# Dilated attention of one mixer: both heads of a unit in turn, scaling on ScalarE, values and the first pair's keys and queries ahead of the mixing

## The chip, the cores and the metric

One Trainium2 chip; the kernel runs on one of its cores. The metric is device time in microseconds, median of several executions. The engines are named as the profile names them: PE (TensorE, matmuls), DVE (VectorE), ACT (ScalarE), POOL (GpSimd), SP (the queue that issues DMAs). Each engine works through its own instructions in order; between engines they wait on semaphores.

## The reference, cut to what matters

Eight layers' halves run one after the other on a (512 tokens, 1024 features) activation. The change lies in one of them, the "even" mixer:

```python
def even_mixer(h, w_in, a_ln_g, a_ln_b, a_ws, a_bs, q_g, k_g, w_out):
    u, v, q, k, vb = split(h @ w_in, [512, 1024, 1536, 2048])
    a_out = chunked_gmlp(gelu(u), gelu(v), a_ln_g, a_ln_b, a_ws, a_bs)   # layer norm of v, causal mixing by a_ws
    qh = rms_norm(heads(q), q_g); kh = rms_norm(heads(k), k_g); vh = heads(vb)   # 8 heads of 64
    for window, dilation in ((128, 1), (512, 4), (2048, 16)):
        o_r, l_r = dilated_branch(qh, kh, vh, window, dilation)   # softmax in the branch's keys
    o = sum over branches of softmax(l_r) * o_r
    return concatenate([a_out, o], -1) @ w_out
```

The kernel computes the three branches at once: a key that lies in n branches counts n times, so that one softmax over all causal keys, with the weight `cnt` (0 to 3) multiplied onto each exponential, gives the same result.

## The kernel before, in words

Activations lie feature by token: 8 tiles of 128x512. Every matrix product is done in three passes (high part times high part, high times low, low times high), so a 128-column block of a projection is 24 matmuls of 512 columns (`mm3`, lines 239 to 241). A weight block is loaded by SP into one of two raw buffers, ACT writes its high part (L213) and DVE the low part (L214). All instructions are written down in a program order, and then a list scheduler puts each engine's instructions into an order of its own from its estimate of the times; what an engine does in which order is therefore not the order of the code.

The even mixer (`even`, L1389) has three parts. `gmlp` projects v by tokens (`token_proj`: 4 weight loads, 96 matmuls, into 4 PSUM banks), projects u in 4 blocks, normalises v and mixes (8 groups of three 256-column matmuls, L1257 to L1259, evicted by ACT, L1260, then 4 transposes, L1264). `dilated` treats 8 heads in 4 pairs. For each pair and each of k, q and v there is a projection of 24 matmuls (`project`, steps P0, P1, P2). For k and q the squares (ACT L1323) are summed per head by small "moments" matmuls (L1326), an inverse root is worked out on DVE in 13 dependent instructions on 128x8 values (L1345 to L1348), for k it is transposed (L1355), copied (L1357), spread over the features by a matmul with `hrow` (L1359) and multiplied in (DVE L1360). For v the projection is scaled by DVE (L1028) and transposed (L1031).

The causal scores of one pair fall into three units, `EVEN_UNITS`: unit 0 is query block 3 (512 keys), unit 1 blocks 0 and 2 (128 and 384 keys), unit 2 block 1 (256 keys). Steps: S makes both heads' scores of a unit in two PSUM banks (L1096, with the mask added by L1094), W makes the weights of one head (`weigh`: DVE maximum L1370, DVE negative scaled maximum L1372, ACT exponential L1373, DVE product with `cnt` and sum L1374, DVE reciprocal L1375, DVE scaling L1376), T transposes weights (PE L1054, ACT L1059, DVE L1060), V multiplies with the values (L1070 to L1075, ACT copy L1077, DVE add L1078). `attention` (L1099) runs the steps of the string `EVEN_STEPS` in each round; the number behind the colon says how many pairs ahead or behind the round's own pair a step works. Transposes and values of a pair stand up to two rounds behind its scores there. A pool of four PSUM banks (`aux`) serves scores, moments and transposes in turn, two banks (`mm`) the projections. Behind the last pair comes the output projection with `ev_wo` (192 matmuls), parts of which the scheduler moves forward.

Of the kernel before, what the change touches and what calls it, by code (L numbers as in the profile page):

```python
# [31 lines left out]
          + [("ba", 4), ("hg", 2)])  # L32
# [25 lines left out]
    "W01:0 S1:0 W00:0 W10:0 T01:-1 T00:0 T21:-1 V0:-2 P0:1 W11:0 S2:0 P2:0 V1:-1 W20:0 T11:0 T20:0 "  # L58
    "W21:0 T10:0 P1:1 S0:1"
# [46 lines left out]
class Kern:  # L106
# [914 lines left out]
    def values(self, ps, vz, scale=None):  # L1021

        nc = self.nc
        vt = self.scr()
        if scale is None:
            nc.scalar.activation(vt, ps, AF.Copy)
        else:
            nc.vector.tensor_mul(vt, ps, scale)  # L1028
# [3 lines left out]
        src = tr.rearrange("p (b d) -> p b d", d=64)  # L1032
        nc.scalar.activation(vz[:, :, 64:128], src, AF.Copy)
        nc.vector.tensor_sub(vz[:, :, 128:192], src, vz[:, :, 64:128])

    def value_tiles(self, n=2):
        res = []
        for k in range(n):
            t = self.pt(f"vz{k}", [P, 8, 192], F32R)
            self.nc.gpsimd.memset(t.bitcast(F32)[:, :, 0:64], 0.0)  # L1040
            res.append(t)
        return res
# [19 lines left out]
    def av(self, s, vz, wts, e):  # L1062
# [4 lines left out]
        for j in range(4):  # L1067
            h, l = (t[:, 4 * j:3 * j + 4].rearrange("p q c -> p (q c)") for t in wts)
            v = vz[:, 2 * j + e]
# [29 lines left out]
    def attention(self, pairs, first, project, weigh, done, mask, order, units):  # L1099
# [5 lines left out]
        for i in range(-2, pairs + 3):  # L1105
            for name, d in steps:
# [5 lines left out]
                if kind == "S":  # L1112
                    s["z", n] = self.scores(s["q"], s["k"], units[n], mask)
                elif kind == "W":
# [15 lines left out]
    def stick(self):  # L1130
        nc = self.nc
        with self.phase("stick") as self.ph:
# [5 lines left out]
            vzs = self.value_tiles()  # L1138
# [57 lines left out]
    def gmlp(self, oh, ol):  # L1196
# [15 lines left out]
        pv = self.token_proj([("ev_v", u) for u in range(4)], self.xh, self.xl)  # L1212
        with self.phase("big") as self.big:
            self.rms_scales()
            early(2)
            self.rms_rows(range(4))
        wr = self.load("wsr", [P, 1024], i["ev_ws"], eng=nc.sync, pool=self.ph)
# [15 lines left out]
        r = self.rstd(var, 4)  # L1233
        for n, v in enumerate(vg):
            V.tensor_scalar(v, v, ag[:, 2 * n:2 * n + 1], r[:, n:n + 1], op0=ALU.subtract, op1=ALU.mult)
# [12 lines left out]
        self.linear(bu[len(pu):], self.xh, self.xl, lambda a, pss: evict(a + len(pu), pss))  # L1248

# [24 lines left out]
    def dilated_masks(self):  # L1274

        nc = self.nc
        ps = self.aux()
        for k, n in enumerate((4, 16)):
            a = self.scr()[0:n, :P]
            nc.gpsimd.memset(a, 0.0)  # L1280
            nc.gpsimd.affine_select(a, a, pattern=[[0, P // n], [-1, n]], compare_op=ALU.not_equal, fill=1.0,
                                    base=0, channel_multiplier=1)
            nc.tensor.matmul(ps[:, :P], a, a, start=k == 0, stop=k == 1)
        cnt = self.pt("cnt")
        for j in range(4):
            nc.scalar.activation(cnt[:, j * P:(j + 1) * P], ps[:, :P], AF.Copy, bias=1.0 if j == 3 else 0.0)
        own = cnt[:, 3 * P:]
        nc.gpsimd.affine_select(own, own, pattern=[[-1, P]], compare_op=ALU.is_ge, fill=0.0, base=0,
                                channel_multiplier=1)
        near = self.scr()[:, :P]  # L1290
        nc.gpsimd.memset(near, 1.0)
        nc.gpsimd.affine_select(near, near, pattern=[[1, P]], compare_op=ALU.is_ge, fill=0.0, base=0,
                                channel_multiplier=-1)
        nc.vector.tensor_add(cnt[:, 2 * P:3 * P], cnt[:, 2 * P:3 * P], near)
        mask = self.pt("dmask", [P, T], BF16)
# [3 lines left out]
    def dilated(self, oh, ol):
        nc, i = self.nc, self.i  # L1300
        V = nc.vector
        cnt, mask = self.dilated_masks()
        gq = self.load("gq", [P, 2], i["ev_qkg"], eng=nc.sync, pool=self.ph)
        gqk = self.pt("gqk", [P, 1])
        V.tensor_mul(gqk, gq[:, 0:1], gq[:, 1:2])
        hsel = self.pt("hsel", [P, 2])
# [3 lines left out]
        hrow = self.pt("hrow", [2, P])  # L1310
        rsq = self.pt("rsq", [P, 104])[:, :4]
# [3 lines left out]
        vzs = self.value_tiles()  # L1315
        bk, bq, bv = (self.simple_blocks(n, 4) for n in ("ev_k", "ev_q", "ev_vb"))

        V.tensor_mul(rsq, self.rcol, self.rcol)

        def moments(ps, st, c0):  # L1320

            sq = self.scr()
            nc.scalar.activation(sq, ps, AF.Square)  # L1323
            for tb in range(4):
                c = c0 + 2 * tb
                nc.tensor.matmul(st[:, c:c + 2], sq[:, tb * P:(tb + 1) * P], hsel, start=True, stop=True)  # L1326

        def project(hp, s, n):

            ps, = self.group([(bk, bq, bv)[n][hp]], self.xh, self.xl)  # L1330
            if n == 2:
                s["v"] = vzs[hp % 2]
                self.values(ps, s["v"], self.rrow)
                return
            st = self.aux()
            moments(ps, st, 0)
            if n == 0:
                kr = self.scr()
                nc.scalar.activation(kr, ps, AF.Copy, scale=gqk)  # L1339
            else:  # L1340
                s["q"] = self.split_psum(ps, "q", 2)
            var = self.small(8)
            per_head = lambda t: t[:, :, None].to_broadcast([P, 4, 2])
            two = lambda t: t.rearrange("p (t e) -> p t e", e=2)
            V.tensor_tensor(two(var), two(st[:, :8]), per_head(rsq), op=ALU.mult)  # L1345
            V.tensor_scalar(var, var, 1e-6, None, op0=ALU.add)
            r = self.rstd(var, 8)
            V.tensor_tensor(two(r), two(r), per_head(self.rcol), op=ALU.mult)  # L1348
            if n == 1:
                s["rq"] = self.small(8)  # L1350
                V.tensor_scalar(s["rq"], r, 0.125, None, op0=ALU.mult)
                return
            tr = self.aux()
            for tb in range(4):
                nc.tensor.transpose(tr[0:2, tb * P:(tb + 1) * P], r[:, 2 * tb:2 * tb + 2], self.ident)  # L1355
            rt = self.pt("rt", [2, T])
            nc.scalar.activation(rt, tr[0:2], AF.Copy)  # L1357
            bc = self.aux()
            nc.tensor.matmul(bc, hrow, rt, start=True, stop=True)  # L1359
            V.tensor_mul(kr, kr, bc)  # L1360
            s["k"] = (self.pt("kh", dt=F32R, bufs=2), self.pt("kl", dt=F32R, bufs=2))
            self.split(kr, *s["k"])

        def weigh(hp, st, z, segs, e):
            p = self.scr()
            for qb, c0 in segs:
                kv = (qb + 1) * P
                zq, pq = z[:, c0:c0 + kv], p[:, c0:c0 + kv]
                mx, nb, den = self.small(1), self.small(1), self.small(1)
                V.reduce_max(mx, zq, axis=AX.X)  # L1370
                sc = st["rq"][:, 2 * qb + e:2 * qb + e + 1]
# [5 lines left out]
            return p  # L1377
# [4 lines left out]
        def first(st):  # L1382
            self.ready = [(0, 0), (0, 1), (0, 2)]
            for hp, n in self.ready:
                project(hp, st[hp], n)

        self.attention(4, first, project, weigh, done, mask, EVEN_STEPS, EVEN_UNITS)

    def even(self):  # L1389
        with self.phase("evout") as self.op:  # L1390
            oh, ol = [None] * NM, [None] * NM
            with self.phase("gmlp") as self.ph:
# [285 lines left out]
    def load_params(self):  # L1678
# [10 lines left out]
        self.ba, self.hg = col["ba"], col["hg"]  # L1689
# [56 lines left out]
def layout(inp):  # L1746
# [10 lines left out]
    par = {"ba": i["od_b_a_2"][0], "hg": i["od_head_g_2"][0]}  # L1757
    for j in (0, 1):
# [22 lines left out]
    d["ev_u"], d["ev_q"], d["ev_k"], d["ev_vb"] = (tiles(w[:, a:a + T]) for a in (0, 1024, 1536, 2048))  # L1781
# [31 lines left out]
```

## Time and profile before

| | us |
|---|---|
| median of 3 runs | 2461.49 (2459.39 to 2463.71) |
| profiled execution | 2465.87 |
| its span, first to last instruction | 2464.1 |
| PE busy in the span | 2392.6 (97%) |
| DVE, ACT busy | 1416.0 (57%), 1003.4 (41%) |

PE is busy nearly everywhere, in the sense that some matmul is under way; matmuls are pipelined and their ends are modelled, so this share hides short stalls. More is seen in the stretches of the even mixer: its first matmul starts at 1255.86 us and that of the next stage at 1502.57 us, and the granted clock of PE is below 1.00 in four of the stretches shown below.

### The profile page before, as it was taken

How to read it: one execution, taken by the hardware profiler on the slowest of the kernel's cores; microseconds unless marked ns; L12 is line 12 of the kernel's file. 1: busy time of each engine (PE TensorE's matmuls, PEld its weight loads, DVE VectorE, ACT ScalarE, POOL GpSimd, SP SyncE). 2: the span in 40 equal slices, each digit the busy share in tenths (PEclk: the TensorE clock that was granted, in tenths of full speed). 3: DMA queues.
4: the chain of work that ended last, by engine and by line, in shares of the span. 5: the costliest groups of instructions: out<-in, count | busy, mean ns of one | idle time of the engine just before them, and what ended most of it. 6: DMA issues, size and time to landing. Idle time of an engine off the chain costs nothing. (4 is left out here: it accounts for less than half of the span.)

```text
span 2464.1 us, 30835 instructions
## 1 busy us (share of the span) xinstructions
PE 2392.6 (97%) x12136; PEld 1987.2 (81%) x12140; DVE 1416.0 (57%) x2560; ACT 1003.4 (41%) x1542; POOL 19.6 (1%) x123
## 2 busy tenths in 40 slices
PE   5899999999999999999999999999999999999999
PEld 4788888888878788888877678888888887888888
DVE  9945633343787863334376886656435677655621
ACT  5843522322665643222254454333225454333311
POOL 0000000000000000000000000000000000000000
PEclk9999999999999999999999999999999999999999
DMA  3532223233221113233322112332332122223231
GB/s 90 110 102 87 86 95 102 92 94 96 78 69 61 52 61 120 94 96 93 99 92 67 44 46 86 112 100 93 94 96 86 52 87 76 94 95 102 90 113 63
DMA packets 99377, 213.49 MB, mean 87 GB/s; under 512 B 44529, under 2 KB 45169, under 8 KB 99233
## 3 DMA queue, kind: packets, MB, share of 16 engines
q1 hardware_dynamic: 99232, 211.53, 27.5%
q8 instruction: 95, 1.56, 0.3%
q14 instruction: 50, 0.40, 0.1%
HBM read 207.04 MB, written 2.10 MB: 85 GB/s over the span
## 5 line engine op out<-in xcount | busy, mean ns | idle before, releaser
L213 ACT ACTIVATE wh<-wr 128x1024 fp32r<-128x1024 f32 (+1 forms) x385 | 400.4, 1041 | 1016.4 <-PE mm L240 401.2
L214 DVE TENSOR_TENSOR wl<-wr,wh 128x1024 fp32r<-128x1024 f32 (+1 forms) x385 | 461.6, 1199 | 440.6 <-ACT wh L213 436.4
L239 PE MATMUL mm<-xh,wh 128*128 128x512 f32 x1016 | 400.5, 394 | 3.5 <-ACT scr L1339 3.1
L240 PE MATMUL mm<-xl,wh 128*128 128x512 f32 x1016 | 400.1, 394 | 0.0
L241 PE MATMUL mm<-xh,wl 128*128 128x512 f32 x1016 | 399.8, 393 | 0.0
L239 PE MATMUL acc<-xh,wh 128*128 128x512 f32 x760 | 296.4, 390 | 0.0
L240 PE MATMUL acc<-xl,wh 128*128 128x512 f32 x760 | 295.9, 389 | 0.0
L241 PE MATMUL acc<-xh,wl 128*128 128x512 f32 x760 | 295.7, 389 | 0.0
L239 PEld LDWEIGHTS mm<-xh,wh 128*128 128x128 f32 x1016 | 192.2, 189 | 45.8 <-ACT scr L1339 3.5
L240 PEld LDWEIGHTS mm<-xl,wh 128*128 128x128 f32 x1016 | 192.2, 189 | 39.6 <-issue 0.2
L241 PEld LDWEIGHTS mm<-xh,wl 128*128 128x128 f32 x1016 | 192.2, 189 | 39.2 <-issue 0.6
L239 PEld LDWEIGHTS acc<-xh,wh 128*128 128x128 f32 x760 | 142.8, 188 | 29.6
L240 PEld LDWEIGHTS acc<-xl,wh 128*128 128x128 f32 x760 | 142.8, 188 | 29.5 <-issue 0.2
L241 PEld LDWEIGHTS acc<-xh,wl 128*128 128x128 f32 x760 | 142.8, 188 | 29.3
L239 PE MATMUL mm<-hh,wh 128*128 128x512 f32 (+1 forms) x396 | 145.0, 366 | 1.0 <-DVE v L353 1.0
L239 PE MATMUL acc<-hh,wh 128*128 128x512 f32 (+1 forms) x396 | 145.1, 366 | 0.5 <-DVE v L353 0.5
L240 PE MATMUL acc<-hl,wh 128*128 128x512 f32 (+1 forms) x396 | 145.1, 366 | 0.0
L240 PE MATMUL mm<-hl,wh 128*128 128x512 f32 (+1 forms) x396 | 145.0, 366 | 0.0
L241 PE MATMUL mm<-hh,wl 128*128 128x512 f32 (+1 forms) x396 | 144.7, 365 | 0.0
L241 PE MATMUL acc<-hh,wl 128*128 128x512 f32 (+1 forms) x396 | 144.7, 365 | 0.0
L239 PEld LDWEIGHTS mm<-hh,wh 128*128 128x128 f32 x396 | 74.7, 189 | 13.5 <-DVE v L353 1.4
L239 PEld LDWEIGHTS acc<-hh,wh 128*128 128x128 f32 x396 | 74.6, 188 | 13.1 <-DVE v L353 0.9
(488 smaller groups left out, 3875.0 us busy)
## 6 DMA issues: line engine op xcount, KB each, us to landing
wr<-down_dram SPq DMA_DIRECT2D x64, 448.0 KB, 3.3
wr<-gu_g_dram SPq DMA_DIRECT2D x44, 512.0 KB, 3.3
wr<-gu_u_dram SPq DMA_DIRECT2D x44, 512.0 KB, 3.3
wr<-gate_dram SPq DMA_DIRECT2D x44, 512.0 KB, 3.3
wr<-up_dram SPq DMA_DIRECT2D x44, 512.0 KB, 3.3
wr<-down_dram SPq DMA_DIRECT2D x32, 512.0 KB, 3.5
wr<-sb_qkv_dram SPq DMA_DIRECT2D x24, 512.0 KB, 3.3
wr<-glu_dram SPq DMA_DIRECT2D x16, 512.0 KB, 3.3
```

What stands on the lines that cost most here:

```text
L213: nc.scalar.activation(hi[:, :cols], raw[:, :cols], AF.Copy)
L214: nc.vector.tensor_sub(lo[:, :cols], raw[:, :cols], hi[:, :cols])
L239: nc.tensor.matmul(ps[:, c0:c1], wh[:, s], xh[k][:, c0:c1], start=st, stop=False)
L240: nc.tensor.matmul(ps[:, c0:c1], wh[:, s], xl[k][:, c0:c1], start=False, stop=False)
L241: nc.tensor.matmul(ps[:, c0:c1], wl[:, s], xh[k][:, c0:c1], start=False, stop=en)
```

## The change

- The value projection of all four pairs is done at once by tokens (`even_values`: 96 matmuls in `token_proj`), ahead of the mixing, scaled per token on eviction; the four projections P2, their scalings (L1028) and 16 transposes (L1031) are gone. The first pair's keys and queries are projected before it, behind the u blocks.
- `weigh` treats both heads of a unit in one step: all maxima, then per part the negative scaled maximum and the exponential, both on ACT, then per part product and reciprocal on DVE and the scaling on ACT.
- `EVEN_STEPS` is another string: all of a pair's steps stand in its own round, and the next pair's projections P0 and P1 behind W1 and W2.
- The layer norm's subtract and scale of v (4 DVE instructions L1235) becomes an ACT activation; masks and constants are made at the start of the mixer, q and k gains come with the parameters instead of a DMA of their own.

```diff
-EVEN_STEPS = ("W01:0 S1:0 W00:0 W10:0 T01:-1 T00:0 T21:-1 V0:-2 P0:1 W11:0 S2:0 P2:0 V1:-1 W20:0 T11:0 T20:0 "
-    "W21:0 T10:0 P1:1 S0:1")
+EVEN_STEPS = ("W0:0 S1:0 W1:0 P0:1 T00:0 T01:0 S2:0 W2:0 P1:1 T10:0 T11:0 T20:0 T21:0 S0:1 V0:0 V1:0")
...
-            V.tensor_scalar(v, v, ag[:, 2 * n:2 * n + 1], r[:, n:n + 1], op0=ALU.subtract, op1=ALU.mult)
+            nc.scalar.activation(v, v, AF.Identity, scale=r[:, n:n + 1], bias=nb[:, n:n + 1])
...
         self.linear(bu[len(pu):], self.xh, self.xl, lambda a, pss: evict(a + len(pu), pss))
+        self.dil_keys(self.ph2, 0)
+        V.tensor_mul(self.rsq, self.rcol, self.rcol)
+        self.pair0 = {}
+        for n in (0, 1):
+            self.dil_project(0, self.pair0, n)
+        self.even_values()
...
+    def even_values(self):
+        pss = self.token_proj([("ev_vb", u) for u in range(4)], self.xh, self.xl)
+        for tb, ps in enumerate(pss):
+            r = self.rcol[:, tb:tb + 1]
+            src = ps.rearrange("p (n d) -> p n d", d=64)
+            h, l = (self.vz[:, tb, :, k:k + 64] for k in (64, 128))
+            nc.scalar.activation(h, src, AF.Copy, scale=r)
+            nc.vector.scalar_tensor_tensor(l, src, r, h, op0=ALU.mult, op1=ALU.subtract)
...
+        if n == 1:
+            s["rq"], s["nrq"] = self.rqs[hp % 2]
+            nc.scalar.activation(s["rq"], r, AF.Copy, scale=0.125)
+            nc.scalar.activation(s["nrq"], r, AF.Copy, scale=-0.125)
+            return
...
-        def weigh(hp, st, z, segs, e):
-            p = self.scr()
-            for qb, c0 in segs:
-                V.reduce_max(mx, zq, axis=AX.X)
-                V.scalar_tensor_tensor(nb, mx, -1.0, sc, op0=ALU.mult, op1=ALU.mult)
-                nc.scalar.activation(pq, zq, AF.Exp, scale=sc, bias=nb)
-                V.scalar_tensor_tensor(pq, pq, 1.0, cnt[:, T - kv:], op0=ALU.mult, op1=ALU.mult, accum_out=den)
-                V.reciprocal(den, den)
-                V.tensor_scalar(pq, pq, den, None, op0=ALU.mult)
+        def weigh(hp, st, zs, segs):
+            ps = [self.scr(), self.scr()]
+            for _, _, z, _, (mx, _, _) in parts:
+                V.reduce_max(mx, z, axis=AX.X)
+            for c, _, z, p, (mx, nb, _) in parts:
+                nc.scalar.activation(nb, mx, AF.Copy, scale=st["nrq"][:, c:c + 1])
+                nc.scalar.activation(p, z, AF.Exp, scale=st["rq"][:, c:c + 1], bias=nb)
+            for _, kv, _, p, (_, _, den) in parts:
+                V.scalar_tensor_tensor(p, p, 1.0, cnt[:, T - kv:], op0=ALU.mult, op1=ALU.mult, accum_out=den)
+                V.reciprocal(den, den)
+                nc.scalar.activation(p, p, AF.Copy, scale=den)
```

Because the scheduler sets each engine's order, three places of it are shown. First ACT in a middle round of the kernel before; `aux` tiles read by L1373 are scores, `mm` tiles are projections, L1323 is the square of the next pair's keys.

```order
L1373 ACTIVATE scr_11861<-aux_11852,small_11863,small_11849 128x512
L1059 ACTIVATE wth_11751<-aux_11918 128x4x128
L213 ACTIVATE wh_12554<-wr_12552 128x1024
L1373 ACTIVATE scr_11889<-aux_11851,small_11891,small_11849 128x512
L1373 ACTIVATE scr_11899<-aux_11871,small_11901,small_11849 128x128
L1077 ACTIVATE scr_11948<-acc_11939 64x512
L1323 ACTIVATE scr_11987<-mm_11961 128x512
```

The square comes behind both heads' exponentials of unit 0 and one of unit 1. Now ACT in a middle round of the changed kernel (its line numbers differ): L1358 and L1359 are the query factors, L1388 the negative scaled maxima, L1389 exponentials, L1393 scalings, L1068 copies of the two heads' value products, L223 the split of the output. First the part on unit 0:

```order
L1358 ACTIVATE misc_10527<-small_11897 128x8
L1359 ACTIVATE misc_10527<-small_11897 128x8
L1388 ACTIVATE small_11972<-small_11971,misc_10527 128x1
L1068 ACTIVATE scr_11950<-acc_11941 64x512
L1388 ACTIVATE small_11975<-small_11974,misc_10527 128x1
L1068 ACTIVATE scr_11962<-acc_11953 64x512
L1389 ACTIVATE scr_11969<-aux_11930,small_11972,misc_10527 128x512
L1389 ACTIVATE scr_11970<-aux_11931,small_11975,misc_10527 128x512
L223 ACTIVATE oh_11965<-scr_11940 128x512
L1393 ACTIVATE scr_11969<-scr_11969,small_11973 128x512
L1393 ACTIVATE scr_11970<-scr_11970,small_11976 128x512
```

and right behind it unit 1 and the square of the next pair's keys (L1337) and their copy (L1345):

```order
L1388 ACTIVATE small_12010<-small_12009,misc_10527 128x1
L1388 ACTIVATE small_12013<-small_12012,misc_10527 128x1
L1389 ACTIVATE scr_12007<-aux_11989,small_12010,misc_10527 128x128
L1389 ACTIVATE scr_12008<-aux_11990,small_12013,misc_10527 128x128
L1388 ACTIVATE small_12016<-small_12015,misc_10527 128x1
L1388 ACTIVATE small_12019<-small_12018,misc_10527 128x1
L1389 ACTIVATE scr_12007<-aux_11989,small_12016,misc_10527 128x384
L1389 ACTIVATE scr_12008<-aux_11990,small_12019,misc_10527 128x384
L1393 ACTIVATE scr_12007<-scr_12007,small_12011 128x128
L1393 ACTIVATE scr_12008<-scr_12008,small_12014 128x128
L1337 ACTIVATE scr_12076<-mm_12051 128x512
```

All 6 exponentials and 4 of 6 scalings of units 0 and 1, for both heads, now stand ahead of the square; two scalings and the copy L1345 follow it. Last, PE in a middle round of the changed kernel, from the moments of the keys (L1341, which read that square) to the spreading of the inverse root (L1367):

```order
L1341 MATMUL aux_11751<-misc_10527,scr_11749 128x2 x4
L238 MATMUL mm_12051<-xh_10214,wh_12047 128x512
L239 MATMUL mm_12051<-xl_10215,wh_12047 128x512
L240 MATMUL mm_12051<-xh_10214,wl_12048 128x512
L238 MATMUL mm_12051<-xh_10216,wh_12047 128x512
L1363 MATMUL aux_11779<-ident_58,small_11776 2x128 x4
L239 MATMUL mm_12051<-xl_10217,wh_12047 128x512
L240 MATMUL mm_12051<-xh_10216,wl_12048 128x512
L238 MATMUL mm_12051<-xh_10218,wh_12047 128x512
L239 MATMUL mm_12051<-xl_10219,wh_12047 128x512
L1367 MATMUL aux_11786<-scr_11784,hrow_10526 128x512
```

Four projection matmuls stand between the moments and the transposes of the inverse root. In the kernel before, the same place of a middle round holds 17 projection matmuls and 6 matmuls of the values.

## Rows read from the trace of the kernel before

**Rows 1.** The page: busy us (share of the span) and instructions by engine.

```profile
PE 2392.6 (97%) x12136; PEld 1987.2 (81%) x12140; DVE 1416.0 (57%) x2560; ACT 1003.4 (41%) x1542; POOL 19.6 (1%) x123
```

**Rows 2.** Busy times by stretch of the even mixer; PEclk is the granted clock.

```profile
core 0: us, PE busy (x) PEld busy (x) DVE busy (x) ACT busy (x) POOL busy (x), PEclk, DMA share, GB/s
1255.86:1314.89 59.03, 54.48 (x238) 42.52 (x237) 53.34 (x141) 37.68 (x70) 1.09 (x1) 0.97 0.28 90
1314.89:1330.02 15.13, 14.85 (x80) 11.19 (x81) 8.54 (x12) 8.30 (x15) 3.28 (x13) 1.00 0.31 105
1330.02:1348.21 18.19, 15.05 (x56) 11.07 (x55) 9.00 (x32) 5.24 (x11) 1.08 (x1) 0.72 0.09 29
1348.21:1375.22 27.01, 25.58 (x135) 18.60 (x135) 20.79 (x79) 13.75 (x25) 0.00 (x0) 1.00 0.18 59
1375.22:1407.76 32.54, 32.21 (x160) 23.37 (x160) 25.87 (x94) 14.98 (x28) 0.00 (x0) 0.90 0.16 50
1407.76:1438.69 30.93, 29.98 (x164) 21.99 (x165) 26.70 (x95) 16.43 (x29) 0.00 (x0) 1.00 0.15 52
1438.69:1467.50 28.81, 26.40 (x142) 19.15 (x143) 23.39 (x82) 13.83 (x27) 0.00 (x0) 1.00 0.05 19
1480.00:1500.00 20.00, 20.00 (x90) 16.58 (x89) 14.96 (x20) 10.73 (x15) 0.00 (x0) 1.00 0.31 106
```

**Rows 3.** Waits of PE, 1314 to 1470 us: total, times, longest.

```profile
PE mm L239 <- ACT scr L1339: 3.1, 1, 3.1
PE aux L1054 <- DVE scr L1376: 2.3, 2, 1.3
```

**Rows 4.** Groups of DVE, 1407.76 to 1438.69 us: busy us, mean ns | idle before.

```profile
L214 DVE TENSOR_TENSOR wl<-wr,wh 128x1024 fp32r<-128x1024 f32 x3 | 3.7, 1223 | 0.0
L1374 DVE SCALAR_TENSOR_TENSOR scr<-scr,cnt 128x512 f32<-128x512 f32 x2 | 1.4, 687 | 0.9 <-ACT scr L1373 0.9
L1375 DVE RECIPROCAL small<-small 128x1 f32<-128x1 f32 x8 | 1.2, 154 | 0.0
L1372 DVE SCALAR_TENSOR_TENSOR small<-small,small 128x1 f32<-128x1 f32 x8 | 1.2, 154 | 0.0
L1376 DVE TENSOR_SCALAR scr<-scr,small 128x512 f32<-128x512 f32 x2 | 1.0, 479 | 0.0
```

**Rows 5.** Groups of ACT by shape, whole span.

```profile
L382 ACT ACTIVATE xh<-v,cst 128x512 fp32r<-128x512 f32 x23 | 16.3, 709 | 0.0
L1077 ACT ACTIVATE scr<-acc 64x512 f32<-64x512 f32 x24 | 14.3, 595 | 8.2 <-PE acc L1075 7.8
L1373 ACT ACTIVATE scr<-aux,small,small 128x512 f32<-128x512 f32 x8 | 6.2, 776 | 16.3 <-DVE small L1372 16.2
L1373 ACT ACTIVATE scr<-aux,small,small 128x384 f32<-128x384 f32 x8 | 5.3, 667 | 0.8 <-DVE small L1372 0.8
L1323 ACT ACTIVATE scr<-mm 128x512 f32<-128x512 f32 x8 | 4.8, 596 | 0.0
L1373 ACT ACTIVATE scr<-aux,small,small 128x128 f32<-128x128 f32 x8 | 3.6, 455 | 13.9 <-DVE small L1372 13.9
L1373 ACT ACT_TABLE_LOAD x1 | 1.3, 1283 | 2.3 <-DVE small L1372 2.3
L1495 ACT ACTIVATE dec<-scr 128x8 f32<-128x8 f32 x4 | 0.9, 216 | 2.3 <-DVE scr L1491 2.2
```

**Rows 6.** Timeline, a longer and a shorter piece: start, us, engine, instruction [idle].

```profile
1330.02 1.05 PE L1326 MATMUL aux<-hsel,scr 128*128 128x2 f32 x8
1334.22 0.79 PE L239 MATMUL mm<-xh,wh 128*128 128x512 f32 x1 [3.14 <-ACT scr L1339]
...
1424.14 0.15 DVE L397 TENSOR_TENSOR small<-small 128x8 f32<-128x8 f32 x1
1424.33 0.17 DVE L398 SCALAR_TENSOR_TENSOR small<-small,small 128x8 f32<-128x8 f32 x1
...
1428.08 1.12 PE L1359 MATMUL aux<-rt,hrow 2*128 2x512 f32 x2
```

More of the change, by code (lines that the diff above doesn't have):

```diff
@@ L414, in colsum @@
         return d
+    ndiag = 4
     def spread(self, rows):
@@ L1113, in attention @@
                     s["z", n] = self.scores(s["q"], s["k"], units[n], mask)
+                elif kind == "W" and len(name) == 2:
+                    s["w", n, 0], s["w", n, 1] = weigh(hp, s, s["z", n], units[n])
                 elif kind == "W":
@@ L1272, in out_pair, with even_consts @@
         return h, l
-    def dilated_masks(self):
+    def even_consts(self):
         nc = self.nc
[L1277 to L1295, printed above, removed]
-        nc.vector.tensor_scalar(mask, cnt, 0.5, -1e30, op0=ALU.is_lt, op1=ALU.mult)
-        return cnt, mask
@@ L1299, in dilated @@
[L1299 to L1306, printed above, removed]
+        cnt, mask = self.pt("cnt"), self.pt("dmask", [P, T], BF16)
+        with self.phase("evt") as ph:
+            ps = self.aux()
+            near = ph.tile([P, P], F32, name=self.nm("near"), tag="near", bufs=1)
+            nc.gpsimd.memset(near, 1.0)
+            nc.gpsimd.affine_select(near, near, pattern=[[1, P]], compare_op=ALU.is_ge, fill=0.0, base=0,
+                                    channel_multiplier=-1)
+            for k, n in enumerate((4, 16)):
+                a = ph.tile([P, P], F32, name=self.nm("sel"), tag="sel", bufs=2)[0:n]
+                nc.gpsimd.memset(a, 0.0)
+                nc.gpsimd.affine_select(a, a, pattern=[[0, P // n], [-1, n]], compare_op=ALU.not_equal, fill=1.0,
+                                        base=0, channel_multiplier=1)
+                nc.tensor.matmul(ps[:, :P], a, a, start=k == 0, stop=k == 1)
+            for j in range(4):
+                nc.scalar.activation(cnt[:, j * P:(j + 1) * P], ps[:, :P], AF.Copy, bias=1.0 if j == 3 else 0.0)
+            own = cnt[:, 3 * P:]
+            nc.gpsimd.affine_select(own, own, pattern=[[-1, P]], compare_op=ALU.is_ge, fill=0.0, base=0,
+                                    channel_multiplier=1)
+            nc.vector.tensor_add(cnt[:, 2 * P:3 * P], cnt[:, 2 * P:3 * P], near)
@@ L1314, in dilated @@
                                 base=0, channel_multiplier=1)
[L1315 to L1362, printed above, removed]
@@ new lines, in dil_keys, with dil_project @@
+    def dil_keys(self, pool, n):
+        self.kq.append([pool.tile([P, T], F32R, name=self.nm(f"{t}{n}"), tag=f"{t}{n}", bufs=1)
+                        for t in ("qh", "ql", "kh", "kl")])
+    def dil_project(self, hp, s, n):
+        nc, V = self.nc, self.nc.vector
+        _, _, hsel, hrow, gqk = self.evc
+        ps, = self.group([self.simple_blocks(("ev_k", "ev_q")[n], 4)[hp]], self.xh, self.xl)
+        sq = self.scr()
+        nc.scalar.activation(sq, ps, AF.Square)
+        st = self.aux()
+        for tb in range(4):
+            nc.tensor.matmul(st[:, 2 * tb:2 * tb + 2], sq[:, tb * P:(tb + 1) * P], hsel, start=True, stop=True)
+        qh, ql, kh, kl = self.kq[hp % 2]
+        if n == 0:
+            kr = self.scr()
+            nc.scalar.activation(kr, ps, AF.Copy, scale=gqk)
+        else:
+            s["q"], s["k"], s["v"] = (qh, ql), (kh, kl), self.vz[:, :, 2 * hp:2 * hp + 2]
+            self.split(ps, qh, ql)
+        var = self.small(8)
+        per_head = lambda t: t[:, :, None].to_broadcast([P, 4, 2])
+        two = lambda t: t.rearrange("p (t e) -> p t e", e=2)
+        V.tensor_tensor(two(var), two(st[:, :8]), per_head(self.rsq), op=ALU.mult)
+        V.tensor_scalar(var, var, 1e-6, None, op0=ALU.add)
+        r = self.rstd(var, 8)
+        V.tensor_tensor(two(r), two(r), per_head(self.rcol), op=ALU.mult)
+        if n == 1:
[3 more added lines that the diff above has]
+            return
+        tr = self.aux()
+        for tb in range(4):
+            nc.tensor.transpose(tr[0:2, tb * P:(tb + 1) * P], r[:, 2 * tb:2 * tb + 2], self.ident)
+        rt = self.scr()[0:2]
+        nc.scalar.activation(rt, tr[0:2], AF.Copy)
+        bc = self.aux()
+        nc.tensor.matmul(bc, hrow, rt, start=True, stop=True)
+        V.tensor_mul(kr, kr, bc)
+        self.split(kr, kh, kl)
@@ L1382, in first @@
         def first(st):
[L1383 to L1387, printed above, removed]
+            self.ready = [(0, 0), (0, 1)]
+            st[0].update(self.pair0)
+        self.attention(4, first, self.dil_project, weigh, done, mask, EVEN_STEPS, EVEN_UNITS)
     def even(self):
-        with self.phase("evout") as self.op:
+        with self.phase("evout") as self.op, self.phase("evc") as self.ph2:
+            self.ph = self.ph2
             oh, ol = [None] * NM, [None] * NM
+            self.kq = []
+            self.even_consts()
+            self.vz = self.pt("vz", [P, 4, 8, 192], F32R)
+            self.nc.gpsimd.memset(self.vz.bitcast(F32)[:, :, :, 0:64], 0.0)
             with self.phase("gmlp") as self.ph:
@@ L1757, in layout @@
     par = {"ba": i["od_b_a_2"][0], "hg": i["od_head_g_2"][0]}
+    par["qg"], par["kg"] = (np.tile(i[f"ev_{n}_g_2"][0], 2) for n in "qk")
     for j in (0, 1):
@@ L1780, in layout @@
     w = i["ev_w_in_2"][0]
[L1781 to L1782 removed]
+    d["ev_u"], d["ev_q"], d["ev_k"] = (tiles(w[:, a:a + T]) for a in (0, 1024, 1536))
+    d["ev_v"], d["ev_vb"] = rows(w[:, T:2 * T]), rows(w[:, 2048:])
     d["ev_ws"] = np.ascontiguousarray(i["ev_a_ws_2"][0].transpose(2, 0, 1).reshape(P, 1024))
```

57 lines of the change are left out of this document (30 added, 27 removed).

## The prediction

> **What bounds the kernel now.** I read the page first. PE has some matmul under way 97% of the span [rows 1], so an edit elsewhere is worth only what PE waits for, or what leaves PE itself; but matmul ends are modelled, so I did not take 97% for "full". Next came the busy times by stretch [rows 2]. In the output projection, which nothing disturbs, 90 matmuls of 512 columns start in 20.00 us: 0.222 us each. That is the price of a PE matmul below; a block of 24 is 5.3 us. The reader should then see in the same rows where the even mixer falls short of it: 18.19 us at a granted clock of 0.72, 32.54 us at 0.90, and an undisturbed middle round of 30.93 us at 1.00. The waits of PE [rows 3] name the cause of the worst place: 3.1 us behind the first keys' copy, at 1330.02 to 1334.22 [rows 6], where ACT, DVE and PE wait for each other in the very first pair. Elsewhere PE waits about 1 us at a time. So two things can move the time: the start of the attention (in this trace bad), and the rounds (in this trace nearly filled by PE).
>
> **What leaves and what moves on PE.** The 96 value matmuls stay 96: 21.3 us, taken out of the rounds and put ahead of the mixing. 16 transposes L1031 go, 0.11 us each by start-to-start, an estimate from a quarter of the 512-column price and the fixed part of a matmul: -1.7 us. A middle round thus holds 30.93 - 5.3 - 0.4 - 1.0 (its own wait) = 24.2 us of PE work. If PE stays the bound, that is what a round will take.
>
> **DVE and ACT in a round.** DVE is busy 26.7 of 30.93 us [rows 2]. It loses 3.0 us of scaling (8 instructions L1376, 0.479 for the widest), 8 L1372 of 0.154 [rows 4], and, for the values, two instructions of L1374's 0.69 us and one weight split L214 of 1.2 us: about 7 us of durations, 6 without their overlaps. It falls to some 21 us. ACT is busy 16.4 us [rows 2]. It loses a weight split and a values copy (1.6 us) and gains 8 scalings and 8 maxima. A scaling by a per-partition operand is not in the trace with these tiles; the same form is L382, 0.709 us at 512 columns [rows 5]; bounds are the DVE price 0.479 and the two-operand exponential 0.776. I take 0.71 less the 0.1 us by which neighbours overlap, 0.6. A 128x1 activation is not in the trace: from below DVE's 0.154 [rows 4], from above the 128-column exponential, 0.455 [rows 5]; nearest is 0.216 for 128x8, plus some 0.08 for the per-partition operand: 0.3 alone, 0.45 for a pair. ACT rises to some 20 us. By sums alone, PE at 24.2 remains the bound.
>
> The Trainium skill says otherwise about the moved scaling: "ScalarE: Activation LUTs", section "Rules for kernel authors", wants multiplications on VectorE rather than ScalarE. Here the row bears it out, 0.479 against 0.709; by that rule the 32 scalings cost some 5 us of engine time more than they save, and that counts where ACT stands in the way.
>
> **Where the order decides.** It stands in the way in the rounds. The next pair's moments on PE read a square that ACT now makes behind all six exponentials and four scalings of two units. I walk a middle round, zero at the end of unit 0's second score matmuls. PE goes on with the rest of the values, 2.0 (5120 columns at 0.222 per 512, less two pieces already done, plus the fixed part of short matmuls), unit 1's scores, 2.2 (two heads, three products and a mask over 512 columns, the same), and 16 projection matmuls, 3.6: it is at the moments at 7.8. ACT copies the second head's value product (L1077's form, 0.595), which PE ends at 2.0, so until 2.6; that copy stands ahead of the exponentials and holds them. Exponentials 2 x 0.7 [rows 5]: 4.0. DVE product 0.69, split of the output 0.6 (an instruction of the same size), reciprocals 0.25 [rows 4]: 5.55. Scalings 2 x 0.6: 6.7. Two maxima 0.45, two 128-column exponentials 0.75, two maxima 0.45, two of 384 columns 1.1, two short scalings 0.6: 10.0. Square 0.6: 10.6. **PE waits 2.8 us.** Then the moments, 1.0 [rows 6]. The four matmuls behind them need the bank that the copy of the keys frees: two scalings and the copy, 1.6 us behind the square, so 0.6 more. The inverse root is 13 dependent instructions at 0.2 us start to start [rows 6], 2.6 us from the end of the moments, of which 1.5 are covered: **1.1 us**. At the next pair's unit 0, the second head's scores need a bank whose last transposes DVE splits behind a 1.2 us weight split and five more: 0.7 us. Small ones, 0.3. Sum 5.5 us: a round takes 29.7, not 24.2. In the kernel before 17 projection matmuls, 3.8 us, stood where four stand now, so the root was hidden.
>
> The first round has the same waits, and the 1.28 us table load of the exponential [rows 5] ahead of them on ACT: 23.8 us from unit 0's scores to the last transposes, of which 5.3 are waits. The last has no next pair, only pieces of the output projection to fill: 17.5 us of work, some 6 us of waits, 23.5.
>
> **The start.** In the kernel before the first 12 matmuls of the keys stand ahead of the mixing at 1314.89, so they start at 1312.2. After: keys and queries 10.7, two moments, transposes and the spreading 3.4 (this time 16 query matmuls hide the root): 14.1. Values 21.3. Mixing with 30 matmuls of the next pair in between: 12.2 (between 11.4 of pure work and 13.4, the 15.13 us of the stretch before less the matmuls it has more). Scores 1.65. Then rounds 23.8 + 2 x 29.7 + 23.5. Sum 156.0: the last values end at 1468.2, against 1467.50 [rows 2], with four more output matmuls done (0.9 us). So at an undisturbed clock **-0.2 us**: the bad start is repaired, and the rounds lose it again. The layer norm on ACT (4 instructions of at most 0.78 us) is hidden by the 33 us that now lie between it and the mixing; without that cover about +1. The constants made early cost DVE 0.7 us in a layer norm that DVE bounds, against a 1.1 us split that moved back; 0, between -0.5 and +0.7. The larger clearing of the values tile (POOL, 2 us) ends long ahead of its use. The dropped DMA was waited for by nobody.
>
> **The clock.** In the kernel before, the one wait of 3.1 us was followed by a mean clock of 0.72 over 18.19 us [rows 2], that is 10.2 us at 1.2 GHz, half of that lost if PE is full: 5 us. Waits of about 1 us were not always followed by any. The first three rounds of the changed kernel each have a wait of about 3 us. Each costs between 0 and 5 us; part of the slow time falls into the other waits, so I take 2: **+6**. The Trainium skill ("TensorE: Matmul & The Clock Gate", section "What's actually happening") holds the low level for the default that only activity lifts; by it the rounds would drop each time, and the traces so far agree after the 3.1 us wait.
>
> **Sum.** 2465.87 - 0.2 + 6 = 2471.7 for an execution like the profiled one, which lay 4.4 above the median; for the median 2461.49 + 5.8 = 2467.
>
> **Rivals.** *The engines keep up* (faster, 0.22). Sums of 21 and 20 us against 24.2 speak for it, and a walk adds up every hop in one order; against it, that ACT's order above cannot be jumped. With rounds of 25.5: 2 x 4.2, 4 in the first, 3 in the last, no clock loss: 2461.5 - 0.2 - 15.4 = 2446. *Walk right, clock holds* (0.22): -0.2, so 2461; the single waits are a little shorter than the one of 3.1 that was punished. *The clock falls in every round as after the first keys before* (slower, 0.16): 3 x 5 us: 2461 + 15 = 2476; it decides from the point where a wait reaches about 3 us. *The forecast* (0.40): 2467, own range 2462 to 2472.
>
> **Chances.** 0.2%, 4.9 us, is about what a measurement of this kernel tells from no change. Two thirds of the forecast and all of the last rival lie above +4.9: 0.43. A third of the forecast and nine tenths of the second: 0.33. The rest, 0.24, is faster. The range 2448 to 2479 reaches into both outer cases and leaves out about 0.2.
>
> **What would show it.** In the profile after: PE waiting at the moments (L1341) for the square (L1337), 2 to 4 us in each of three rounds, and about 1 us at the transposes L1363 for DVE; rounds of 28 to 31 us; the 3.1 us wait at the first keys gone; the first scores near 1360; the clock below 1.00 in the rounds and 1.00 through values and mixing. The forecast is wrong if PE does not wait at L1341 (then the faster rival), or if the clock stays at 1.00 in the rounds.

## The result, and the profile after

The changed kernel takes 2480.91 us (median of 4 runs, 2478.97 to 2482.84), the kernel before 2460.54 beside it: a ratio of 1.0073, 95% interval [1.006, 1.0085]. It is slower by 20 us; the forecast was slower by 6. In a later batch the same code came to 1.0089 [1.0072, 1.0105].

First the busy times by stretch of the changed kernel, columns as in [rows 2]. The stretches are: layer norm, gated unit and table; keys and queries of the first pair; all values; mixing; then four rounds, cut behind the last transposes of each.

```profile
core 0: us, PE busy (x) PEld busy (x) DVE busy (x) ACT busy (x) POOL busy (x), PEclk, DMA share, GB/s
1257.20:1316.10 58.90, 53.04 (x230) 41.89 (x229) 50.05 (x138) 38.58 (x74) 3.56 (x3) 0.94 0.28 90
1316.10:1330.09 13.99, 13.97 (x65) 10.33 (x63) 8.32 (x22) 6.63 (x10) 0.00 (x0) 1.00 0.34 112
1330.09:1352.94 22.85, 22.85 (x105) 19.02 (x105) 10.05 (x22) 6.83 (x11) 0.00 (x0) 1.00 0.21 70
1352.94:1365.50 12.56, 12.56 (x71) 9.48 (x69) 7.94 (x11) 7.82 (x15) 0.00 (x0) 1.00 0.27 85
1365.50:1393.75 28.25, 23.61 (x117) 16.18 (x116) 16.55 (x58) 17.77 (x37) 0.00 (x0) 0.88 0.11 38
1393.75:1425.26 31.51, 27.74 (x140) 18.98 (x138) 21.23 (x75) 19.84 (x46) 0.00 (x0) 0.95 0.10 34
1425.26:1459.18 33.92, 30.56 (x134) 20.44 (x132) 21.32 (x75) 19.67 (x47) 0.00 (x0) 0.80 0.10 32
1459.18:1482.33 23.15, 21.01 (x110) 14.20 (x108) 16.33 (x59) 16.33 (x43) 0.00 (x0) 1.00 0.00 1
```

The reader should see three things. The start is now smooth: PE is busy through keys, values and mixing at a clock of 1.00, where [rows 2] had 18.19 us at 0.72 (one of three stretches there below 1.00, not four). The sums are as forecast: in a middle round DVE is busy 21.2 us, ACT 19.8. And still a middle round lasts 31.5 and 33.9 us, no less than the 30.93 of before, although 24 value matmuls (5.3 us) left it.

What PE waits for in the four rounds (total, times, longest), to be laid beside [rows 3]:

```profile
PE aux L1341 <- ACT scr L1337: 9.5, 5, 3.8
PE aux L1045 <- ACT scr L1393: 1.1, 2, 0.8
PE mm L238 <- ACT scr L1345: 1.1, 2, 0.5
PE aux L1363 <- DVE small L1355: 0.9, 2, 0.6
```

L1341 are the moments, L1337 is the square they read. Why that square is late stands in ACT's timeline of the second round (start, us, instruction):

```profile
1404.83 1.34 ACT L1393 ACTIVATE scr<-scr,small 128x512 f32<-128x512 f32 x2 [0.93 <-DVE small L1392]
1406.07 0.47 ACT L1388 ACTIVATE small<-small,misc 128x1 f32<-128x1 f32 x2
1406.44 0.79 ACT L1389 ACTIVATE scr<-aux,small,misc 128x128 f32<-128x128 f32 x2
1407.13 0.47 ACT L1388 ACTIVATE small<-small,misc 128x1 f32<-128x1 f32 x2
1407.50 1.22 ACT L1389 ACTIVATE scr<-aux,small,misc 128x384 f32<-128x384 f32 x2
1408.61 0.69 ACT L1393 ACTIVATE scr<-scr,small 128x128 f32<-128x128 f32 x2
1409.19 0.59 ACT L1337 ACTIVATE scr<-mm 128x512 f32<-128x512 f32 x1
1409.67 1.12 ACT L1393 ACTIVATE scr<-scr,small 128x384 f32<-128x384 f32 x2
1410.68 0.68 ACT L1345 ACTIVATE scr<-mm,misc 128x512 f32<-128x512 f32 x1
```

PE starts the last projection matmul at 1406.8; the square starts at 1409.19, behind the second unit's weights, and the keys' copy L1345, which frees the bank, later still. ACT never rests from 1404.83 on.

On PE the three waits for the keys' squares, one in each of the first three rounds, look like this (in brackets the idle time before):

```profile
1377.20 1.56 PE L1341 MATMUL aux<-misc,scr 128*128 128x2 f32 x8 [3.84 <-ACT scr L1337]
...
1409.84 1.05 PE L1341 MATMUL aux<-misc,scr 128*128 128x2 f32 x8 [2.65 <-ACT scr L1337]
...
1441.34 1.05 PE L1341 MATMUL aux<-misc,scr 128*128 128x2 f32 x8 [2.65 <-ACT scr L1337]
```

And all of the half clock in the rounds, that is time at the lower of PE's two clock levels, lies in three stretches, each of which begins within 2 us of the end of one of these waits (columns as in [rows 2]):

```profile
1377.50:1384.50 7.00, 6.39 (x20) 4.28 (x20) 3.32 (x14) 2.76 (x5) 0.00 (x0) 0.51 0.11 37
1411.50:1415.50 4.00, 3.71 (x12) 2.28 (x12) 2.81 (x12) 1.40 (x2) 0.00 (x0) 0.57 0.00 0
1442.00:1456.50 14.50, 13.90 (x42) 8.49 (x42) 7.85 (x26) 6.48 (x14) 0.00 (x0) 0.53 0.11 37
```

### The profile page after: what moved, and what is told of

The parts are those of the page before. It is cut to its first block, busy times and chain, and to the rows that moved or that the text cites. A ratio compares the mean times of both kernels' runs of the same rounds, so it can differ in the third digit from the quotient of the medians.

```text
span 2477.0 us, 30790 instructions
## 1 busy us (share of the span) xinstructions
PE 2399.0 (97%) x12124; PEld 1990.6 (80%) x12124; DVE 1400.4 (57%) x2485; ACT 1026.8 (41%) x1618; POOL 20.4 (1%) x122
## 5 line engine op out<-in xcount | busy, mean ns | idle before, releaser
L238 PE MATMUL mm<-xh,wh 128*128 128x512 f32 x984 | 386.4, 393 | 1.1 <-ACT scr L1345 0.5
L239 PE MATMUL mm<-xl,wh 128*128 128x512 f32 x984 | 385.9, 392 | 0.0
L240 PE MATMUL mm<-xh,wl 128*128 128x512 f32 x984 | 385.2, 391 | 0.0
L238 PEld LDWEIGHTS mm<-xh,wh 128*128 128x128 f32 x984 | 185.4, 188 | 41.6 <-issue 2.1
L240 PEld LDWEIGHTS mm<-xh,wl 128*128 128x128 f32 x984 | 185.3, 188 | 38.6 <-issue 0.9
L239 PEld LDWEIGHTS mm<-xl,wh 128*128 128x128 f32 x984 | 185.3, 188 | 38.5
```

Source lines behind the costliest of these rows:

```text
L238: nc.tensor.matmul(ps[:, c0:c1], wh[:, s], xh[k][:, c0:c1], start=st, stop=False)
L239: nc.tensor.matmul(ps[:, c0:c1], wh[:, s], xl[k][:, c0:c1], start=False, stop=False)
L240: nc.tensor.matmul(ps[:, c0:c1], wl[:, s], xh[k][:, c0:c1], start=False, stop=en)
```

## Experiments

Theory A: PE waits at the moments because the square stands in ACT's queue behind weights that nobody needs yet, and these waits bring the half clock. Theory B: the chain scores, weights, transposes bounds the round, and the wait at the moments only shows its slack. All ratios are to the kernel before, runs of the same batch.

The table gives, for each profiled execution, the stretch from the first recorded mask matmul of the scores to the start of the last value matmul, with its mean granted clock. Medians are over all runs, the last two columns from one execution each.

| kernel | median us | ratio, 95% interval | scores to values, us | clock |
|---|---|---|---|---|
| before | 2460.5 to 2464.6 by batch | 1 | 118.14 | 0.97 |
| changed | 2480.91 | 1.0073 [1.006, 1.0085] | 116.17 | 0.90 |
| e1 keys first | 2464.13 | 0.9996 [0.9987, 1.0006] | 99.13 | 0.97 |
| e2 no wait for the square | 2473.53 | 1.0041 [1.0027, 1.0054] | 113.64 | 0.88 |
| e3 waits filled | 2479.24 | 1.0061 [1.0048, 1.0074] | 111.83 | 0.98 |
| e4 scaling on DVE | 2483.02 | 1.0077 [1.0064, 1.0091] | 117.66 | 0.91 |
| e5 moments a step of their own | 2467.09 | 1.0008 [0.9999, 1.0017] | 99.44 | 0.93 |
| e6 old rounds | 2492.35 | 1.0109 [1.0094, 1.0125] | 126.86 | 0.79 |
| e7 keys first, maxima on DVE | 2459.18 | 0.998 [0.9971, 0.9989] | 94.81 | 1.00 |
| e8 e1, table split on GpSimd | 2461.94 | 0.9992 [0.9983, 1.0001] | 99.13 | 0.97 |
| e9 e7, constants late | 2459.15 | 0.9987 [0.9977, 0.9996] | 96.02 | 0.98 |
| e10 e7, values carried | 2462.37 | 0.9997 [0.9988, 1.0006] | 100.23 | 0.95 |
| e11 changed again | 2486.13 | 1.0089 [1.0072, 1.0105] | 122.54 | 0.85 |

**e1.** One step changes its place.

```diff
-    "W0:0 S1:0 W1:0 P0:1 T00:0 T01:0 S2:0 ..."
+    "W0:0 S1:0 P0:1 W1:0 T00:0 T01:0 S2:0 ..."
```

> One step is moved: the next pair's key projection (with its square) is issued ahead of the weights of the second unit instead of behind them, so ScalarE makes the square right behind the first unit's exponentials. Theory A (the square is queued on ScalarE behind six exponentials and scalings, TensorE waits for it, and the waits take the clock down): the 2.8 to 4 us waits at the moments and the 0.6 us behind them go, 3 x 3.3 = 10 us, and some 8 us of half clock with them: 2463 us (2456 to 2470), about 18 below the changed kernel's 2481. Theory B (a round lasts as long as the chain scores - weights - transposes, and the wait at the moments is only where the slack shows): the wait reappears at the transposes of the weights and the time stays at 2478 to 2483.

ACT of e1 at the same place of the round:

```profile
1395.12 1.45 ACT L1389 ACTIVATE scr<-aux,small,misc 128x512 f32<-128x512 f32 x2
1396.46 0.63 ACT L223 ACTIVATE oh<-scr 128x512 fp32r<-128x512 f32 x1
1396.98 0.59 ACT L1337 ACTIVATE scr<-mm 128x512 f32<-128x512 f32 x1
1397.46 0.69 ACT L1345 ACTIVATE scr<-mm,misc 128x512 f32<-128x512 f32 x1
```

Its waits of PE, from the mixing to the end of the stage:

```profile
PE aux L1341 <- ACT scr L1337: 2.1, 3, 0.8
```

The stretch in the changed kernel, and in e1:

```profile
1365.94:1482.11 116.17, 102.27 (x493) 69.48 (x492) 75.01 (x263) 73.41 (x169) 0.00 (x0) 0.90 0.08 28
1365.46:1464.59 99.13, 94.29 (x493) 66.29 (x492) 73.02 (x263) 71.76 (x169) 0.00 (x0) 0.97 0.10 33
```

The square and the copy now follow the first exponentials, the waits at the moments fall from 9.5 to 2.1 us, and the stage loses 17 us. The instructions are the same (493 matmuls, 263 of DVE, 169 of ACT in either stretch), so their number and their sums explain nothing; the order does. The scheduler moved PE's order along: the last projection matmul starts 5.1 us behind unit 0's scores instead of 8.3, and PE still waits less, because the square starts 5.7 us behind them instead of 10.7. Theory A holds, B falls.

**e2.** The square is computed, but nobody reads it.

```diff
-  ... matmul(st[:, 2 * tb:2 * tb + 2], sq[:, tb * P:(tb + 1) * P], hsel, ...)
+  ... matmul(st[:, 2 * tb:2 * tb + 2], self.evc[0][:, tb * P:(tb + 1) * P], hsel, ...)
```

> The moments read the table of counts, which is long there, instead of the square, so the mean squares of queries and keys are left out; the square is still computed and read by nobody. All else as in the changed kernel. Theory A: the three waits at the moments (9.5 us in the trace) go and nothing takes their place, the chain of the inverse root starts earlier and is hidden too (1 us a round), and the clock stays up: 2460 us (2453 to 2468). Theory B: the time stays at 2477 to 2483, with new waits of PE at the transposes or scores.

Waits of PE in its rounds:

```profile
PE mm L238 <- ACT scr L1345: 6.7, 3, 3.4
```

The wait at the moments is gone but for one of 0.9 us, and 6.7 of its 9.5 us stand one step later, at the bank that the keys' copy frees: that copy is behind the same weights. So 7 us were gained by the medians, not 20, and the clock fell as before (0.88, in the slowest of its six executions). The time lies between what A and B expected. A missed it: it is the queue that holds PE, by whatever reader of the projection, not the square alone.

**e3.** Twelve matmuls without a reader in the wait.

```diff
+        for k in range(12 if n == 0 and hp else 0):
+            nc.tensor.matmul(st[:, 8:], self.xh[0][:, :P], self.xh[0][:, 8:], start=True, stop=True)
```

> Twelve matmuls of 504 columns (2.6 us) whose product nobody reads are added ahead of each of the three later key moments, in the place where TensorE waits. If idle TensorE in these waits is what lowers its clock (theory A's second half), the half-clock stretches of the rounds (23.9 us in the profiled execution) go, the waits shrink below 1 us, and the time falls although work was added: 2472 us (2466 to 2476). If the clock falls for another reason, the time stays within 2479 to 2484 and the stretches remain.

The stretch of e3, columns as above:

```profile
1367.73:1479.56 111.83, 102.15 (x529) 70.89 (x528) 75.10 (x263) 73.73 (x169) 0.00 (x0) 0.98 0.08 29
```

Its two parts, and its largest waits of PE (L1343 and L1365 are the moments and transposes in its numbering):

```profile
1367.73:1454.00 86.27, 78.62 (x411) 54.77 (x410) 57.62 (x200) 56.99 (x125) 0.00 (x0) 1.00 0.11 37
1454.00:1460.00 6.00, 6.00 (x25) 3.71 (x26) 4.03 (x19) 2.04 (x6) 0.00 (x0) 0.72 0.00 0
```

```profile
PE aux L1343 <- ACT scr L1337: 3.6, 5, 1.8
PE aux L1365 <- DVE small L1357: 2.4, 3, 1.0
```

The clock stays up, 0.98 against 0.90 and (e11) 0.85, and the stretch is 4 to 11 us shorter with 36 matmuls (some 8 us) more in it. Its only half clock begins at about 1455 us, behind the longest wait that is left: 1.8 us at the queries' moments, which were not filled. Over all its runs the mean granted clock is 0.989 to 0.993, in the changed kernel's first four 0.987 to 0.991. The time falls by less than expected and lies in the range of the other branch (1.0061 overlaps the changed kernel's interval): 3.6 us of waits at the moments stay, 2.4 of them at the queries', and 2.4 at the transposes. That the half clock in the rounds comes with these waits is shown by this profile; the gain in time is at the edge of what the runs can tell. Nor is a long wait the only way to it: in the kernel before, the granted clock is 0.54 from 1377.0 to 1384.5 us, and the longest wait of PE in the 10 us ahead of that is 0.3 us.

**e4.** Scaling back on DVE: one part of the change undone.

```diff
-                nc.scalar.activation(p, p, AF.Copy, scale=den)
+                V.tensor_scalar(p, p, den, None, op0=ALU.mult)
```

> The scaling by the reciprocal sum goes back to VectorE, nothing else changes. By the engine sums (and by the Trainium skill's rule that multiplications belong on VectorE, page ScalarE: Activation LUTs) ScalarE is 3.8 us a round lighter, so the square comes some 2.4 us earlier and three waits shrink: 2473 us (2468 to 2477). Rival: the scalings then stand on VectorE ahead of the maxima of the next unit, the exponentials wait for those, and the square stays as late as it was: 2480 to 2486.

DVE and ACT of e4 in the second round:

```profile
1405.48 0.87 DVE L1393 TENSOR_SCALAR scr<-scr,small 128x512 f32<-128x512 f32 x2
1406.27 1.22 DVE L1386 TENSOR_REDUCE small<-aux 128x1 f32<-128x128 f32 x3
```

```profile
1405.60 0.29 ACT L1388 ACTIVATE small<-small,misc 128x1 f32<-128x1 f32 x1 [1.18 <-DVE small L1386]
1406.59 0.30 ACT L1388 ACTIVATE small<-small,misc 128x1 f32<-128x1 f32 x1 [0.70 <-DVE small L1386]
...
1409.42 0.59 ACT L1337 ACTIVATE scr<-mm 128x512 f32<-128x512 f32 x1
```

Its largest wait of PE in the rounds:

```profile
PE aux L1341 <- ACT scr L1337: 14.6, 6, 4.0
```

ACT is 13 us lighter over the stage (60.4 against 73.4) and the keys' square in this round hardly earlier, 10.4 us behind the scores of unit 0 instead of 10.7: the scalings now stand on DVE in front of three maxima, ACT waits 1.9 us for those ahead of the exponentials, and the square follows them. Over the stage PE even waits longer at the moments, 14.6 us against 9.5, because waits at the queries' moments were added (3.0 and 3.6 us). The rival was right; what the load is on one engine says little when two engines hand work to each other in order.

**e6.** The new start with the old rounds: weights of one head at a time, scaling and maxima on DVE.

```diff
-    "W0:0 S1:0 W1:0 P0:1 T00:0 T01:0 S2:0 W2:0 P1:1 T10:0 T11:0 T20:0 T21:0 S0:1 V0:0 V1:0"
+    "W01:0 S1:0 W00:0 W10:0 T01:-1 T00:0 T21:-1 V0:-2 P0:1 W11:0 S2:0 V1:-1 W20:0 T11:0 T20:0 W21:0 T10:0 P1:1 S0:1"
```

> The changed kernel's start (values and first pair ahead of the mixing, constants early) with the old rounds: the weights of one head at a time, scaling and maxima on VectorE, the old order of steps without its value projections. If TensorE bounds the old rounds, they lose the 5.3 us of each value projection: 118 - 21 = 97 us from the first scores to the last values, and the time is some 2459 us (2453 to 2465), below before. If the old rounds are held by VectorE and ScalarE (26.7 of 30.9 us busy before, 24 without the value split) and by the waits between heads, the value matmuls were their filling: 112 to 118 us in the rounds, 2476 to 2486.

The stretch in the kernel before and in e6, and the largest waits of PE in e6:

```profile
1348.87:1467.01 118.14, 113.18 (x593) 82.37 (x595) 96.10 (x344) 57.98 (x106) 0.00 (x0) 0.97 0.14 45
1366.19:1493.05 126.86, 107.11 (x487) 74.66 (x486) 87.93 (x327) 54.08 (x104) 0.00 (x0) 0.79 0.08 26
```

```profile
PE aux L1045 <- DVE scr L1388: 10.6, 10, 2.4
PE aux L1045 <- DVE small L1384: 3.2, 3, 1.1
```

Ten waits at the transposes for DVE's scaled weights (in [rows 3] two, 2.3 us): this points to the value matmuls that left the rounds as what PE had done in that time. The old rounds without them took 9 us longer than with them, 126.86 against 118.14, at a clock of 0.79, and longer than either branch expected. The two rows part this roughly. PE's idle time is 19.8 us against 5.0, 15 us more; its busy time fell by 6.1 us although value matmuls of 21.3 us left, so the lower clock cost an estimated 15. So the new rounds were needed for the new start, and gained 10.7 us over the old ones there, even with their waits.

**e5, e7, e10: versions meant to beat both.** e7 is e1 with the maxima on DVE:

```diff
-                nc.scalar.activation(nb, mx, AF.Copy, scale=st["nrq"][:, c:c + 1])
+                V.scalar_tensor_tensor(nb, mx, -1.0, st["rq"][:, c:c + 1], op0=ALU.mult, op1=ALU.mult)
```

> Keys first, and the shifted maxima back on VectorE (8 instructions of 0.15 us a round there instead of 8 of 0.28 on ScalarE). Theory A: ScalarE, whose queue decides, is some 1.5 us a round lighter: 2461 us (2458 to 2463) against 2464 with keys first alone. Rival, as with the scalings: VectorE makes them behind other work, the exponentials wait, and the time is the same or longer: 2464 to 2468.

The stretch of e7:

```profile
1365.80:1460.61 94.81, 89.92 (x494) 63.05 (x492) 74.88 (x295) 66.72 (x137) 0.00 (x0) 1.00 0.10 34
```

It beats both kernels, 0.2% below the one before. Theory A's price is met, but its reason is not shown: PE waits 2.1 us at the moments in e7 as in e1, and what differs in the profiles is the clock. 0.97 over 99.13 us is some 6 us of half clock, an estimated 2.8 of the 4.3 us that the stretch is shorter (by 0.47 us for each, see e11). e10 has e7's instructions and this order, e5 also makes the moments a step of their own (M) and the low part of the table on GpSimd:

```diff
# e10
+    "V1:-1 S1:0 W0:0 P0:1 T00:0 W1:0 S2:0 W2:0 T01:0 P1:1 T10:0 T11:0 T20:0 T21:0 V0:0 S0:1"
# e5
+    "P0:1 S1:0 W0:0 M0:1 W1:0 S2:0 P1:1 W2:0 M1:1 T01:0 T10:0 T00:0 S0:1 T11:0 T20:0 V1:-1 T21:0 V0:0"
+                elif kind == "M":
+                    self.dil_norm(hp, s, n)
```

> As keys first with the maxima on VectorE, but the second head's values are carried into the next round and the first transposes stand ahead of the second unit's weights. Theory A (each wait of TensorE that is covered by a carried piece counts in full): some 2 us less, 2457. Rival (the carried pieces push short matmuls together, and the clock falls in the rounds as in the best-order run): 2460 to 2466.

> A version meant to beat both: the moments of keys and queries are a step of their own, so matmuls of other steps can stand between a projection and its moments; the key projection is issued first in a round; the second head's values move behind the next pair's scores; the shifted maxima go back to VectorE; the low part of the mixing table is made by GpSimd, out of the way of the layer norm's sums. Theory A (what TensorE waits for in a round is ScalarE's queue, and shortening that queue and covering each wait with other matmuls is worth its full length): the 0.9 us waits at the moments left in the run before go in most rounds, the eight maxima leave ScalarE (some 1.8 us a round), 1.1 us of the layer norm: 2464 - 8 = 2456 us (2450 to 2461). Theory B (the chain scores - weights - transposes bounds the round from here on): no better than keys first alone, 2461 to 2466.

Neither is better than e7, and both miss theory A's forecast; for e10 the time and the clock came as its rival said, for what reason was not tested. PE waits no more at the moments than in e7 (2.1 us in all there, 1.5 in e10, 1.3 in e5, none over 0.8), and yet the clock is lower, 0.95 and 0.93. Why it falls there, and in e1 behind a wait of 0.7 us, and not in e7 with like waits, stays open.

**e8, e9: the layer norm.** In the changed kernel PE waits 2.2 us for its last sums (L410), 1.1 before. e8 changes `self.split(wr, wsh, wsl)` to `self.split(wr, wsh, wsl, nc.gpsimd)`; e9 calls even_consts() ahead of dil_keys instead of at the start.

> Keys first, and the low part of the mixing table made by GpSimd instead of VectorE. In the changed kernel's layer norm TensorE waits 2.35 us for the last sums of VectorE, 1.25 before; the split of this table (1.2 us on VectorE) stands ahead of them. If that split is the difference, the wait is back at 1.2 us and the time 1.1 us lower (2463); if the masks and constants made early are the cause, the wait stays at 2.3 us and the time at 2464.

> Keys first with the maxima on VectorE (2459 before), and the masks and small constants of the attention made behind the layer norm instead of ahead of the gated unit. If their 0.7 us on VectorE and their place in the queues are what delays the layer norm's last sums, the wait there falls from 2.35 to about 1.2 us and the time to 2458; if the delay is the split of the mixing table (which on GpSimd did not help), the wait stays at 2.3 us and the time at 2459.

The wait is 1.9 us in e8 and 2.2 in e9, so the constants are not its cause. Whether the split is, e8 cannot tell, because GpSimd held DVE up (below).

**e11.** The changed kernel once more.

> The changed kernel once more, beside the runs of this batch. If the half clock in its rounds belongs to it, a new profile shows 15 to 30 us of half clock between the first scores and the last values again, in stretches behind the waits at the moments; if it was chance, under 10 us. Ratio to the kernel before 1.006 to 1.0085 again.

```profile
1367.10:1489.64 122.54, 106.74 (x488) 72.99 (x490) 74.94 (x263) 73.44 (x169) 0.00 (x0) 0.85 0.08 26
```

A mean of 0.85 over 122.54 us is 2 x 0.15 x 122.54 = 36.8 us of half clock; the first profile had 2 x 0.10 x 116.17 = 23.2 (23.9 by its three stretches above). That is more than the 15 to 30 expected, and again it stands behind the waits: the mean clock is 0.57, 0.55 and 0.57 from 1378 to 1394, 1412 to 1431 and 1450 to 1458 us. It belongs to the kernel. One code, two executions: 13.6 us more of half clock go with 6.4 us more, 0.47 us each. The Trainium skill (TensorE: Matmul & The Clock Gate, section "Terms") puts the penalty at half of the throttled time where the clock is halved; here the trace agrees. As a price the 0.47 is an estimate: 1.9 of the 6.4 us are longer idle time of PE, and the clocks are rounded to 0.01.

## Why the prediction was right in its sign and short in its size

The mechanism came as forecast, PE waiting at the moments for a late square and losing clock behind that; the size did not, 20 us instead of 6. The stated range ended at 2479: the median of 2480.91 lies 2 us above that, and the ratio put on the forecast's base of 2461.49 gives 2479.5.

- **The waits: right.** The walk gave 2.8 us at the moments; the second and third round show 2.65, the first 3.84. The bank's 0.6 is 0.5 in the trace. The root's 1.1 is 0.6, and the 0.7 us at the second head's scores is not there.
- **The prices: right.** A scaling of 512 columns takes 0.718 us (0.71 taken from L382 of [rows 5]), a 128x1 maximum 0.286 (0.3), and the sums of DVE and ACT are met. So the first rival, that the engines keep up, failed as the prediction said: by ACT's order. With the work in another order e1 and e7 come near its rounds (99.13 and 94.81 us; its sum, cut the same way, is 92.3), though not its time, 2464 and 2459 against 2446.
- **The rounds without the clock: 2 us too long.** At an estimated 0.47 us each, the 23.2 us of half clock cost 10.9, so the stretch is 105.3 undisturbed; the walk's 1.65 + 23.8 + 2 x 29.7 + 23.5, cut the same way (0.66 less at the ends), is 107.7.
- **The clock: the step that failed.** "Each costs between 0 and 5 us ... so I take 2: +6". By the same estimate it cost 10.9 us in the profiled execution and 17 in its repeat, a mean of 3.6 to 5.8 a wait, and single waits differ much: behind the three stood 6.9, 3.4 and 13.6 us of half clock, some 3.2, 1.6 and 6.4 us. The mechanism was right, this term of the sum was sized too small. The rival with three full losses (2476) came nearer. Reading the one punished wait of 3.1 us as the rule would have been better than halving it.
- **The start: 4 us short.** First scores 104.1 us behind the first value projection of the gated unit were forecast (1360 less 1255.86), 108.3 came. Of this 1.1 is the longer wait for the layer norm's sums, costed at 0; keys, queries and values took 36.8 together, not 35.4 (the 22.85 us stretch of the values also holds the queries' moments and the spreading); half clock in the stretch (0.94 against 0.97 [rows 2]) took about 1.7 (7.1 us against 3.5, at 0.47 each).
- **From the profile to the median: 6 us.** The forecast took 4.4 us off, as the profiled execution of before lay that much above its median. The one of after lay 1.9 below its own. With the 7.3 us between 2471.7 and the profiled 2479.0 (1.3 of them in the unchanged work ahead of the stage) that is 13.6 of the 13.9 us missed.
- **What was not asked:** what the value matmuls did in the rounds. The prediction priced them at 5.3 us a round as if their time would be free; e6 points to their having been cover.

## What to carry to other kernels

Before you move matmuls out of a loop, ask which wait they cover: in e6 the loop without them was 9 us longer. Where an in-order engine feeds PE, put what PE needs next ahead of what it needs later, and judge that by the queue's order, not by busy sums; one token of an order was worth 17 us here. Here a wait of about 3 us on a PE that is otherwise full cost its length and, by estimate, some 4 to 6 us more on average for the half clock behind it.

## What the hardware showed unexpectedly

GpSimd is no free place for a subtraction. In e8 it takes the table's split, and a DVE subtraction that starts under it takes 2.57 us instead of 1.22:

```profile
1283.13 2.39 POOL L224 TENSOR_TENSOR wsl<-wsr,wsh 128x1024 fp32r<-128x1024 f32 x1 [11.94 <-ACT wsh L223]
```

```profile
1284.03 2.57 DVE L213 TENSOR_TENSOR wl<-wr,wh 128x1024 fp32r<-128x1024 f32 x1 [0.29 <-ACT wh L212]
```

It ends 1.1 us behind the end of GpSimd's, as if it had begun only there (spans on GpSimd are rough). The Trainium skill (SBUF — State Buffer, section "SBUF: two separate sides") says that an instruction of VectorE with two inputs in SBUF and one of GpSimd that reads SBUF lock each other out for their whole length; the trace agrees.
